# Two tiles of the branch projection's sum T2 trade places, and the two cache copies move behind the down projection's last residual addition

## The chip, the core and the metric

The kernel runs on one core of a Trainium2 chip. The core has five engines that each execute their own instructions in order: TensorE (PE) multiplies matrices, VectorE (DVE) and ScalarE (ACT) do elementwise work, GpSimd (POOL) and SyncE (SP) here do little but issue transfers. Transfers run on 16 DMA engines, which the queues of POOL (q0 in the profile) and SP (q1) share. Engines wait for each other through semaphores. The metric is the device time of one execution in microseconds (us), the median of several runs.

## The reference

One step of a hybrid decoder layer in float32, for a prompt of 1024 tokens and a decode batch of 8 x 8 tokens, 1088 columns in all; the model is 1024 wide, the feed-forward part 2816.

```
xn = RMSNorm(x)
q, k, v, glu_a, glu_b, gate_a, gate_b = split(xn @ w_in)
A = window_attention(q, k, v, sinks) @ w_o_attn            # window 128, caches k_past, v_past
c = LayerNorm(causal_conv31(glu_a * sigmoid(glu_b)))
B = silu(c) @ w_pb                                         # the branch projection
h = x + (sigmoid(gate_a) * A + sigmoid(gate_b) * B) @ w_out
gate, val = split(causal_conv3(RMSNorm(h) @ w_up))
y = h + (silu(gate) * val) @ w_down
outputs: RMSNorm(y); the last 128 keys and values of the prompt and of the decode batch; the convolutions' last rows
```

For the decode batch the new key and value windows are `concat(k_past, k_new)[-128:]`: 120 old positions are copied from the caches, and 8 are new. The copy of the old positions depends on nothing that the kernel computes.

## The kernel before, in words

A float32 product is made of three matmuls on reduced words: every operand is split into a high word (a cast on ACT, L227) and a low word (a subtraction on DVE, L228: the source less its cast), and `mm3` (L192 to L194) issues high x high, then the same weight with the data's low word, then the weight's low word. A "product" below is a run of such triples into one or two banks of PSUM, evicted by ACT or DVE.

The stages follow one another: the input projection, convolution and attention; the attention's out projection (`do_o`), the branch projection, the out projection, the up projection with its convolution (`ffn_up`), and the down projection (`ffn_down`). A scheduler that orders the rows of each engine when the kernel is built, from the program and its dependencies, sets the order of the work. `issue_after(x)` says that an instruction stands behind x.

*The branch projection.* Two output blocks are computed as seven products in place of eight, on sums of quarters of the data. `ln_apply` makes the sums T1 and T2 as words in SBUF and stores others to memory. `t_split` (L1048 to L1061) splits T1 to T3 into tiles called t{x}{j}{y}: x is the sum (0 is T1, 1 is T2, 2 is T3), j the half of the columns, y the word (0 high, 1 low). The tiles are allocated beforehand, in an order that a table gives:

```
at = {}
for tag in T_PLACES:
    at[tag] = self.t(tb, [P, KT // 2, QW], "t" + tag, F32R)
```

The order decides only at which place in SBUF a tile lies, and thus whose last use of that place it waits for. Some of the places were held before by `ma`, the gated result of the attention's out projection, which POOL stores to memory (L1011).

*The up projection.* It works through pairs of blocks, seven products a pair. `up_start(f)` prepares a row buffer `st` for the convolution: a memset and a copy on POOL (L1378, L1383), and, at f = 5 only, the two DMA copies of the caches between them (L1381, L1382). Each weight operand is split into `whi` and `wlo`, halves 0 and 1.

*The down projection.* `H`, the result, collects additions on DVE (L1690 in this part). `product(s, hooks)` works again in seven products for each row block m, on sums of the weights: `a_load` brings raw weights `ar` on SP's queue (L1631), `a_prep` adds two of them to `as` (L1644) and splits into `aw`, three products ahead (A_AHEAD = 3). `residual(m)` is a DMA on POOL's queue which adds the stored h to H:

```
def residual(m):
    nc.gpsimd.dma_start(H[:, m], self.d_h[m], accum_op=ALU.add)
```

`hooks` calls such steps at a place (m, p) of the product; the last two residuals (m = 3 and 7) are called at (0, 0) of `product(1)`.

Of the kernel before, what the change touches and what calls it, by code (L numbers as in the profile page):

```python
# [9 lines left out]
ALU = mybir.AluOpType  # L10
# [7 lines left out]
NT = 8  # L18
# [23 lines left out]
AHEAD = 3  # L42
UP_LATER = 100
GATE_AFTER = 30
T_PLACES = ("000", "001", "200", "201", "210", "100", "211", "111", "010", "011", "101", "110")
SPLIT_AFTER = 4
GATE_LATER = 60
DOWN = ((0, 1), (2, 3), (16, 17), (18, 19, 20, 21))
# [74 lines left out]
class Build:  # L123
# [898 lines left out]
    def phase_z(self, s_es, sp, xw, sb):  # L1022
# [40 lines left out]
# [3 lines that stand above are left out]
# [267 lines left out]
    def ffn_up(self, hh, hl, mp):  # L1333
        nc, tc, a, pool = self.nc, self.tc, self.a, self.pool
# [40 lines left out]
        def up_start(f):  # L1375
            st = self.t(ft, [P, FW], "st", bufs=4)
            ss = st[:, 2 + SEQ:].rearrange("p (b t) -> p b t", b=NB)
            z = nc.gpsimd.memset(st[:, 0:2], 0.0)  # L1378
            if f == 5:
                with tc.issue_after(z.ins):  # L1380
                    nc.gpsimd.dma_start(a["o_kwp"], a["kpT"][:, :, :, NT:])  # L1381
                    nc.gpsimd.dma_start(a["o_vwp"], a["vp"][:, NT:, :])  # L1382
            nc.gpsimd.tensor_copy(ss[:, :, 0:2], co[:, f, 2:].rearrange("p (b t) -> p b t", b=NB))  # L1383

            def parts(c):
                o, n = QUARTERS[c]
                m = min(n, SEQ - o)
                yield st[:, 2 + o:2 + o + m], lambda v: v[:, :m]
                if m < n:
                    yield ss[:, :, 2:], lambda v: v[:, m:n].rearrange("p (b t) -> p b t", b=NB)  # L1390

            def ev(c, o, n, ps):
                for d, r in parts(c):
                    nc.scalar.copy(d, r(ps))
            return st, ss, parts, ev
# [40 lines left out]
        def plain(f):  # L1436
            fs = (f, NF + f)
            ws = [self.weight(("up", x), 2 - n if f == 0 else 1) for n, x in enumerate(fs)] if f == 0 else [None] * 2
            both = [up_start(x) for x in fs]
            if f == 0:  # L1440
                for c in range(4):
                    for w, b in zip(ws, both):
                        self.stream(None, xs, b[3], chunks=(c,), w=w, table=QUARTERS)
            else:
                for x, b in zip(fs, both):
                    self.stream(("up", x), xs, b[3], chunks=range(4), table=QUARTERS)
            if f == 0:
                with self.later(-60):
                    sums()
            finish(f, both, PLAIN_LATER)  # L1450
# [75 lines left out]
        def pair(f):  # L1526
            base = 7 * (f - PLAIN)
            (_, _, pg, _), (_, _, pv, _) = both = [up_start(x) for x in (f, NF + f)]
            banks = {}
            copy = nc.scalar.copy  # L1530
# [82 lines left out]
    def ffn_down(self, mp):  # L1613
        nc, a = self.nc, self.a
        h_es, a_es, s_es, d_es = [ExitStack() for _ in range(4)]
        H = self.t(self.pool(h_es, "hd", "left"), [P, KT, T], "H")
# [17 lines left out]
        def a_prep(n):  # L1634
            add = nc.vector.tensor_tensor
            while len(tiles) < min(n, 56):
                p = len(tiles) % 7
                a11, a21, a12, a22 = raws[len(tiles) // 7]
                r = {0: a11, 5: a12, 6: a22}.get(p)
                if r is None:  # L1640
                    sums[p] = r = self.t(aw, [P, 3, P], "as", bufs=3)
                    x, y, op = ((a21, a22, ALU.add), (a11, sums.get(1), ALU.subtract), (a12, sums.get(2), ALU.add),
                                (a21, a11, ALU.subtract))[p - 1]
                    add(r, x, y, op)  # L1644
                t = self.t(aw, [P, 3, 2, P], "aw", F32R, bufs=A_AHEAD + 2)
                self.split_ps(t[:, :, 0, :], t[:, :, 1, :], r)
                tiles.append(t)
                a_load()
# [16 lines left out]
        gated = lambda f: self.g_split(f, self.g_load(f, row()), mp)  # L1665

        def residual(m):
            nc.gpsimd.dma_start(H[:, m], self.d_h[m], accum_op=ALU.add)

        seq = (("A", True, 0, 0), ("E", True, 4, 2), ("A", False, 0, 2), ("E", False, 0, 2), ("A", False, 4, 2),  # L1670
               ("C", True, 0, 0), ("A", False, 4, 0))
# [1 line left out]
        def product(s, hooks):  # L1673
            for m in range(4):
                banks = {}
                for p, (bank, fresh, row, c) in enumerate(seq):
                    n = 28 * s + 7 * m + p
                    a_prep(n + 1 + A_AHEAD)
                    w = tiles[n]
                    for j in range(2):  # L1680
                        if fresh:
                            banks[bank, j] = self.bank("mm" if bank == "A" else "aux")
                        ps = banks[bank, j][:, :QW]
                        cs = slice(j * QW, (j + 1) * QW)
                        for x in range(3):
                            b = ops[s, p, x]
                            self.mm3(ps, w[:, x, 0], w[:, x, 1], b[:, 0, cs], b[:, 1, cs], fresh and x == 0, x == 2,
                                     not fresh)
                        hs = H[:, row + m, (c + j) * QW:(c + j + 1) * QW]
                        self.added = nc.vector.tensor_tensor(hs, hs, ps, ALU.add).ins  # L1690
                    for go in hooks.get((m, p), ()):
                        go()

        def each(f, xs):
            return [lambda x=x: f(x) for x in xs]
# [25 lines left out]
        for m in range(3):  # L1721
            hooks.setdefault((m, 6), []).extend(each(residual, (m, m + 4)))
        product(0, hooks)
        late = {divmod(2 * x, KT): [lambda i=x + 10: second(i)] for x in range(11)}
        late[2, 2] = [lambda: a_prep(28 + A_AHEAD + 2)] + late[2, 2]
        self.down(2, H, None, late)
        product(1, {(0, 0): each(residual, (3, 7)), (2, 0): [unit], (2, 2): [unit], (2, 4): each(gated, (18,)),
                    (2, 6): each(gated, (19,)), (3, 0): each(gated, (20,)), (3, 1): [unit] + each(gated, (21,)),
                    (3, 2): [unit]})
        a_es.close()  # L1730
# [191 lines left out]
```

## Time and profile before

| | us |
|---|---|
| median of 3 runs | 1653.63 (1653.21 to 1654.59) |
| profiled execution | 1655.33 |
| its span | 1653.5 |
| PE busy | 1641.8 (99%) |
| DVE busy | 1372.9 (83%) |
| ACT busy | 865.5 (52%) |
| POOL busy | 260.3 (16%) |
| mean granted PE clock | 0.998 |

The profile lists, for the profiled execution, groups of instructions by engine, line of the program, operation and tile names (output<-input, buffer numbers left out), with their busy time, and the idle time of the engine before them with the instruction that ended it. A row of a timeline gives the start, the duration, the engine, the line, and in brackets the idle time before and its releaser. A row of a window gives busy times of PE, PE's weight loads, DVE, ACT and POOL with the counts of instructions, then the granted clock, the share of the 16 DMA engines and GB/s. Matmuls overlap, so two starts lie closer than one duration. A store or load is shown at its issue; "DMA to landing" is the time from the issue until it has arrived.

### The profile page before, as it was taken

The page shows a single profiled execution, that of the slowest core. Times are in us where ns is not written, and L with a number is a line of the kernel's source. Part 1 is how long each engine was busy: PE and PEld are TensorE (multiplying, and loading weights), DVE is VectorE, ACT ScalarE, POOL GpSimd, SP SyncE. Part 2 cuts the span into 40 slices and gives each one's busy share as a digit, 9 for nine tenths or more (in the row PEclk, how much of TensorE's full clock was granted, in tenths as well). Part 3 has the DMA queues.
Part 4 walks back from the last instruction along what each step waited for, and adds up shares of the span by engine and source line. Part 5 has one row for each costly group of instructions (what it writes and reads, how often), then busy time and mean ns, then how long its engine had stood idle before and what let it go on. Part 6 is the DMA issues. An engine that isn't in the chain of part 4 may idle for free. (4 is left out here: it accounts for less than half of the span.)

```text
span 1653.5 us, 30189 instructions
## 1 busy us (share of the span) xinstructions
PE 1641.8 (99%) x11606; PEld 1625.1 (98%) x11606; DVE 1372.9 (83%) x2474; ACT 865.5 (52%) x1795; POOL 260.3 (16%) x551
## 2 busy tenths in 40 slices
PE   9999999999999999999999999999999999999998
PEld 9999999999999999999999999999999999999997
DVE  7899979999979996787755887698888787989867
ACT  6524378774488845585533454454444454524222
POOL 0100112221011111121003421142222110000000
PEclk9999999999999999999999999999999999999999
DMA  6221222223121255647763533243333334766403
GB/s 209 84 66 47 65 71 75 94 98 96 51 61 45 86 204 178 199 162 195 194 223 105 186 110 127 77 137 114 116 109 115 98 100 135 259 162 164 109 14 109
DMA packets 102497, 200.48 MB, mean 121 GB/s; under 512 B 23904, under 2 KB 54640, under 8 KB 102336
## 3 DMA queue, kind: packets, MB, share of 16 engines
q1 hardware_dynamic: 78864, 128.52, 25.0%
q0 software_dynamic: 23056, 69.75, 14.2%
q8 instruction: 91, 1.49, 0.4%
q14 instruction: 54, 0.44, 0.1%
q10 hardware_dynamic: 432, 0.27, 0.1%
HBM read 136.44 MB, written 64.03 MB: 121 GB/s over the span
## 5 line engine op out<-in xcount | busy, mean ns | idle before, releaser
L192 PE MATMUL mm<-xh,whi 128*128 128x384 f32 (+1 forms) x904 | 301.3, 333 | 0.0
L193 PE MATMUL mm<-xl,whi 128*128 128x384 f32 (+1 forms) x904 | 295.4, 327 | 0.2
L194 PE MATMUL mm<-xh,wlo 128*128 128x384 f32 (+1 forms) x904 | 295.5, 327 | 0.0
L193 PEld LDWEIGHTS mm<-xl,whi 128*128 128x128 f32 x904 | 170.0, 188 | 1.6 <-DVE xl L279 0.8
L192 PEld LDWEIGHTS mm<-xh,whi 128*128 128x128 f32 x904 | 169.9, 188 | 0.7
L194 PEld LDWEIGHTS mm<-xh,wlo 128*128 128x128 f32 x904 | 169.7, 188 | 0.1
L1403 DVE SCALAR_TENSOR_TENSOR acc<-st,fc,acc 128x1104 f32<-128x1104 f32 x88 | 119.9, 1364 | 3.7 <-ACT acc L1401 2.4
L173 ACT CAST whi<-wraw 128x1024 fp32r<-128x1024 f32 (+1 forms) x65 | 62.7, 970 | 72.9 <-PE mm L193 52.7
L227 ACT CAST whi<-wraw 128x512 fp32r<-128x512 f32 x84 | 52.6, 626 | 77.0 <-PE aux L194 36.9
L227 ACT CAST wlo<-wraw 128x512 fp32r<-128x512 f32 x84 | 52.6, 626 | 73.5 <-PE aux L194 41.3
L522 DVE SCALAR_TENSOR_TENSOR bt<-u,consts,bt 128x513 f32<-128x513 f32 x120 | 89.7, 747 | 0.7
L522 DVE SCALAR_TENSOR_TENSOR c<-sm,hsum,c 128x512 f32<-128x512 f32 x120 | 89.5, 746 | 0.7
L192 PE MATMUL mm<-mh,whi 128*128 128x272 f32 (+4 forms) x296 | 88.2, 298 | 0.0
L194 PE MATMUL mm<-mh,wlo 128*128 128x272 f32 (+4 forms) x296 | 87.9, 297 | 0.0
L228 DVE TENSOR_TENSOR wlo<-wraw,wlo 128x512 fp32r<-128x512 f32 x84 | 60.7, 723 | 29.0 <-ACT wlo L227 27.8
L522 DVE SCALAR_TENSOR_TENSOR c<-u,consts,c 128x512 f32<-128x512 f32 x112 | 83.5, 746 | 0.6
L193 PE MATMUL mm<-ml,whi 128*128 128x272 f32 (+4 forms) x280 | 82.9, 296 | 0.0
L228 DVE TENSOR_TENSOR whi<-wraw,whi 128x512 fp32r<-128x512 f32 x84 | 58.2, 694 | 28.3 <-ACT whi L227 27.2
L174 DVE TENSOR_TENSOR wlo<-wraw,whi 128x1024 fp32r<-128x1024 f32 (+1 forms) x65 | 72.6, 1121 | 8.6 <-ACT whi L173 7.2
L1555 ACT COPY st<-mm 128x272 f32<-128x272 f32 (+2 forms) x140 | 46.8, 350 | 54.4 <-PE mm L194 54.4
L192 PE MATMUL aux<-mh,whi 128*128 128x272 f32 (+4 forms) x232 | 69.7, 300 | 0.0
L193 PE MATMUL mm<-tl,wlo 128*128 128x272 f32 x240 | 69.6, 290 | 0.0
(652 smaller groups left out, 5741.3 us busy)
## 6 DMA issues: line engine op xcount, KB each, us to landing
wraw<-wall SPq DMA_DIRECT2D x118, 512.0 KB, 4.2
bw<-d_b SPq DMA_DIRECT2D x42, 272.0 KB, 4.0
d_b<-gd POOLq DMA_DIRECT2D x36, 272.0 KB, 6.1
d_b<-acc POOLq DMA_DIRECT2D x24, 272.0 KB, 3.7
ar<-wdn SPq DMA_DIRECT2D x32, 192.0 KB, 3.5
d_g<-acc POOLq DMA_DIRECT2D x10, 544.0 KB, 5.0
ga<-d_ga SPq DMA_DIRECT2D x8, 544.0 KB, 4.8
ct<-d_c SPq DMA_DIRECT2D x8, 544.0 KB, 5.6
```

Source lines behind the costliest of these rows:

```text
L173: self.cast = self.nc.scalar.copy(h[:, z], r[:, z]).ins
L174: self.nc.vector.tensor_tensor(l[:, z], r[:, z], h[:, z].bitcast(F32), ALU.subtract)
L192: mm(ps, wh, xh, start=first, stop=False, skip_group_check=more)
L193: mm(ps, wh, xl, start=False, stop=False, skip_group_check=more)
L194: self.last_mm = mm(ps, wl, xh, start=False, stop=last, skip_group_check=more).ins
L227: self.cast = self.nc.scalar.copy(h, src).ins
L228: self.low = self.nc.vector.tensor_tensor(l, src, h.bitcast(F32), ALU.subtract).ins
L522: mac = lambda o, x, w: nc.vector.scalar_tensor_tensor(o, x, w, o, ALU.mult, ALU.add)
L1403: nc.vector.scalar_tensor_tensor(acc, st[:, k:k + AW], fw(f, k), acc, ALU.mult, ALU.add)
L1555: op(d, r(ps))
```

## The change: what it does

Three edits: in the table of places, T2's low word of the second half (`111`) and T3's (`211`) trade their positions; the two cache copies leave `up_start`; and they are issued by a new hook behind the residual of row block 7, on the same queue. Lines after the first removed ones shift by four (L1644 is L1640 in the new program, L1690 is L1686).

```diff
-T_PLACES = ("000", "001", "200", "201", "210", "100", "211", "111", "010", "011", "101", "110")
+T_PLACES = ("000", "001", "200", "201", "210", "100", "111", "211", "010", "011", "101", "110")
...
         def up_start(f):
             st = self.t(ft, [P, FW], "st", bufs=4)
             ss = st[:, 2 + SEQ:].rearrange("p (b t) -> p b t", b=NB)
-            z = nc.gpsimd.memset(st[:, 0:2], 0.0)
-            if f == 5:
-                with tc.issue_after(z.ins):
-                    nc.gpsimd.dma_start(a["o_kwp"], a["kpT"][:, :, :, NT:])
-                    nc.gpsimd.dma_start(a["o_vwp"], a["vp"][:, NT:, :])
+            nc.gpsimd.memset(st[:, 0:2], 0.0)
             nc.gpsimd.tensor_copy(ss[:, :, 0:2], co[:, f, 2:].rearrange("p (b t) -> p b t", b=NB))
...
         def residual(m):
-            nc.gpsimd.dma_start(H[:, m], self.d_h[m], accum_op=ALU.add)
+            self.rest = nc.gpsimd.dma_start(H[:, m], self.d_h[m], accum_op=ALU.add).ins
...
-        product(1, {(0, 0): each(residual, (3, 7)), (2, 0): [unit], (2, 2): [unit], (2, 4): each(gated, (18,)),
+
+        def windows():
+            with self.tc.issue_after(self.rest):
+                nc.gpsimd.dma_start(a["o_kwp"], a["kpT"][:, :, :, NT:])
+                nc.gpsimd.dma_start(a["o_vwp"], a["vp"][:, NT:, :])
+
+        product(1, {(0, 0): each(residual, (3, 7)) + [windows], (2, 0): [unit], (2, 2): [unit], (2, 4): each(gated, (18,)),
```

DVE's rows in the branch projection, where the low words of T2 are written; the names are tile, buffer number and, in brackets, what a row waits for (DMASW is the landing of a POOL transfer, DMAHW of an SP transfer, Activation is ACT):

```order
 L228 TENSOR_TENSOR t101_1039_7959<-w1_942_7286,t100_1034_7954 128x4x136 [waits Activation_49]
-L228 TENSOR_TENSOR t111_1036_7956<-w2_975_7547,t110_1040_7960 128x4x136 [waits DMASW7_49,DMASW5_49,Activation_49]
-L228 TENSOR_TENSOR t111_1036_7956<-w3_1005_7786,t110_1040_7960 128x4x136 [waits Activation_49]
+L228 TENSOR_TENSOR t111_1035_7955<-w2_975_7547,t110_1040_7960 128x4x136 [waits DMASW5_49,Activation_49]
+L228 TENSOR_TENSOR t111_1035_7955<-w3_1005_7786,t110_1040_7960 128x4x136 [waits Activation_49]
 L228 TENSOR_TENSOR wlo1_1049_7990<-wraw_1010_7833,wlo1_1049_7990 128x512 [waits Activation_49]
```

The rows keep their order, and t111 loses its wait for one of two POOL transfers. Ten rows on, T3's low word has it:

```order
-L228 TENSOR_TENSOR t211_1035_7955<-mh11_1026_7943,t210_1033_7953 128x544 [waits DMAHW0_49,Activation_49]
-L228 TENSOR_TENSOR t211_1035_7955<-mh11_1026_7943,t210_1033_7953 128x544 [waits Activation_49]
+L228 TENSOR_TENSOR t211_1036_7956<-mh11_1026_7943,t210_1033_7953 128x544 [waits DMAHW0_49,DMASW7_49,Activation_49]
+L228 TENSOR_TENSOR t211_1036_7956<-mh11_1026_7943,t210_1033_7953 128x544 [waits Activation_49]
 L228 TENSOR_TENSOR whi1_1058_8103<-wraw_1010_7833,whi1_1058_8103 128x512 [waits PE_49,Activation_49]
```

So the wait has moved with the place. In the up projection, in the pair of blocks behind the copies, PE's rows are these before, at the end of the product on the weight tile `wlo0_1364`:

```order
L193 MATMUL aux_1379_11817<-tl01_1237_10195,wlo0_1364_11677 128x272
L194 MATMUL aux_1379_11817<-th01_1229_10187,wlo0_1364_11677 128x272
L192 MATMUL aux_1386_11931<-mh01_1196_9665,wlo0_1380_11832 128x272 [waits DVE_49,Activation_49]
L193 MATMUL aux_1386_11931<-ml01_1198_9667,wlo0_1380_11832 128x272
L192 MATMUL aux_1387_11945<-mh11_1205_9821,wlo0_1380_11832 128x272 [waits DVE_49]
```

The product on `wlo0_1380`, which is a further tile of the name wlo0, follows at once. The same place of the new program, and 72 rows on:

```order
L193 MATMUL aux_1379_11815<-tl01_1237_10195,wlo0_1364_11675 128x272
L194 MATMUL aux_1379_11815<-th01_1229_10187,wlo0_1364_11675 128x272
L192 MATMUL mm_1375_11770<-th10_1230_10188,whi1_1367_11707 128x272 [waits Activation_49]
...
L193 MATMUL mm_1376_11784<-tl21_1241_10199,whi0_1377_11798 128x272
L194 MATMUL mm_1376_11784<-th21_1233_10191,whi0_1377_11798 128x272
L192 MATMUL aux_1386_11929<-mh01_1196_9665,wlo0_1380_11830 128x272
L193 MATMUL aux_1386_11929<-ml01_1198_9667,wlo0_1380_11830 128x272
```

Three products (on whi1_1367, wlo1_1374 and whi0_1377) now stand between the two, which is the order that every other pair has before and after. Last, the end of POOL's rows, before:

```order
L1668 DMA H_15734<-d_h_64 128x1088 [waits DMASW5_49,DVE_49]
L1668 DMA H_15734<-d_h_64 128x1088 [waits DMASW6_49,DVE_49]
L1668 DMA H_15734<-d_h_64 128x1088 [waits DMASW7_49,DVE_49]
L1668 DMA H_15734<-d_h_64 128x1088 [waits DMASW0_49,DVE_49]
L1901 UNCONDITIONAL_BRANCH
```

and after:

```order
L1664 DMA H_15732<-d_h_64 128x1088 [waits DMASW5_49,DVE_49]
L1664 DMA H_15732<-d_h_64 128x1088 [waits DMASW6_49,DVE_49]
L1726 DMA o_kwp<-kpT 2048x120 [waits DMASW7_49]
L1727 DMA o_vwp<-vp 8x2x15360 [waits DMASW0_49]
L1903 UNCONDITIONAL_BRANCH
```

The copies stand behind the eighth residual as the last transfers on POOL; each waits for an older POOL transfer whose semaphore it uses again (the one eight transfers before it). SP's rows have the same order in both programs.

## The prediction

> **What bounds the kernel now.** I read the busy times first, then the list of what TensorE (PE) waited for, then timelines of each engine around those waits, and last the transfers around the place to which the copies go.
>
> ```profile
> PE 1641.8 (99%) x11606; PEld 1625.1 (98%) x11606; DVE 1372.9 (83%) x2474; ACT 865.5 (52%) x1795; POOL 260.3 (16%) x551
> ...
> PE mm L193 <- DVE t L228: 1.6, 1, 1.6
> ...
> PE aux L192 <- ACT wlo L227: 0.8, 1, 0.8
> ```
>
> PE is busy for 99% of the span and no matmul is added or removed. So the time moves only where PE stops, and an edit elsewhere counts as far as it opens or closes a stop. The two waits quoted (instruction, whom it waited for, then total, times and longest in us) are the ones that the change can touch. Of the other five one is the second step of the first stop below, and four stand where order and waits stay as they are.
>
> **The stop at T2.** PE's timeline (start, duration, instruction, and in brackets idle time and releaser), then windows of it (busy times, then PE's clock, DMA share and GB/s):
>
> ```profile
> 745.02 0.29 PE L194 MATMUL aux<-t,whi 128*128 128x272 f32 x1
> ...
> 745.78 0.29 PE L192 MATMUL mm<-t,wlo 128*128 128x272 f32 x1
> 747.63 0.39 PE L193 MATMUL mm<-t,wlo 128*128 128x272 f32 x1 [1.56 <-DVE t L228]
> 748.23 0.39 PE L194 MATMUL mm<-t,wlo 128*128 128x272 f32 x1 [0.21 <-DVE wlo L228]
> 748.46 0.29 PE L192 MATMUL mm<-t,wlo 128*128 128x272 f32 x1
> ...
> 749.70:752.90 3.20, 3.20 (x16) 3.20 (x15) 3.20 (x6) 3.20 (x8) 0.40 (x1) 0.50 0.54 165
> ```
>
> From 745.02 to 745.78 the starts are six steps apart, 0.127 us each. The next three starts come 1.85, 0.60 and 0.23 us apart, so 1.72 + 0.47 + 0.10 = 2.3 us are lost. Two microseconds later the granted clock is 0.50 for 3.2 us: 16 matmuls take 3.2 us instead of 16 x 0.127 = 2.0, a loss of 1.2, or of 1.6 if I take half of the 3.2. I take 1.4. The stop costs 3.7 us together.
>
> Who is late there? VectorE (DVE), ScalarE (ACT) and GpSimd (POOL), with the landing times of the two stores:
>
> ```profile
> 743.26 0.71 DVE L228 TENSOR_TENSOR t<-w,t 128x544 fp32r<-128x544 f32 x1
> 746.22 1.36 DVE L228 TENSOR_TENSOR t<-w,t 128x544 fp32r<-128x544 f32 x2 [2.25 <-ACT ml L1153]
> 747.50 0.68 DVE L228 TENSOR_TENSOR wlo<-wraw,wlo 128x512 fp32r<-128x512 f32 x1
> ...
> 738.99 2.29 ACT L227 CAST t<-w 128x544 fp32r<-128x544 f32 x4 [0.49 <-DVE ma L1010]
> ...
> 738.22 0.56 POOL L1011 DMA_DIRECT2D d_ma<-ma  x1 [2.29 <-DVE ma L1010]
> ...
> DMA to landing us min/median/max: 4.3/4.3/4.3
> ...
> 739.74 0.61 POOL L1011 DMA_DIRECT2D d_ma<-ma  x1
> ...
> DMA to landing us min/median/max: 6.4/6.4/6.4
> ```
>
> DVE stands idle for 2.25 us before it writes T2's low part t111. The releaser named is ACT, but the casts that t111 needs (four in one row) were done by 741.3. What ends at that moment is a store: `ma` issued at 739.74 lands 6.4 later, at 746.1, and t111 lies where that `ma` lay. So DVE waits for a store to leave the place, and PE waits for DVE.
>
> **The change, part by part.**
>
> *T2 and T3 trade places.* No instruction is added or moved; one wait goes from t111's row to that of T3's low part t211. t111 keeps its wait for the earlier store (738.22 + 4.3 = 742.5) and for the casts, both over when DVE ends the row of 743.26. So the two t111 halves start at about 743.9 and 744.5 and the row of wlo follows at 745.2 and ends near 745.85, just ahead of PE, which would ask for it from 745.9 to 746.05. t211 comes after the rows quoted, later than 746.1, so its new wait should cost nothing; if T3 came earlier, it would inherit the stop. I take a gain of 3.6 of the 3.7 (0.1 for a wlo that comes a touch late); the least is 2.3, if a small stop or the clock loss stays.
>
> *The copies leave POOL's row between two memsets.* A stop in the up projection, 46 us behind the copies, belongs to this edit:
>
> ```profile
> 1063.68 0.29 PE L194 MATMUL aux<-th,wlo 128*128 128x272 f32 x1
> 1064.73 0.39 PE L192 MATMUL aux<-mh,wlo 128*128 128x272 f32 x1 [0.76 <-ACT wlo L227]
> 1064.96 0.29 PE L193 MATMUL aux<-ml,wlo 128*128 128x272 f32 x1
> ...
> 1065.21 0.29 PE L193 MATMUL aux<-ml,wlo 128*128 128x272 f32 x1
> 1065.46 0.39 PE L194 MATMUL aux<-mh,wlo 128*128 128x272 f32 x1
> ...
> 1064.06 0.62 ACT L227 CAST wlo<-wraw 128x512 fp32r<-128x512 f32 x1 [2.40 <-PE aux L194]
> ...
> 1066.00:1070.00 4.00, 4.00 (x34) 4.00 (x34) 4.00 (x4) 1.85 (x4) 0.93 (x2) 1.00 0.47 135
> ```
>
> PE loses 0.92 + 0.10 + 0.13 = 1.15 us up to 1065.46, and about 0.1 behind it: 1.25. The product that starts at 1064.73 uses wlo0_1380, which lies where wlo0_1364 lay, and PE's order (shown with the change) has it right behind the product on wlo0_1364. So ACT's cast into that place waits 2.40 us for the last matmul of that product, and PE waits for the cast. In the new order three products of 24 matmuls, some 9 us at 0.127 each, stand between the two, and the cast has that time. The clock stayed at 1.00 here, so nothing more is to be had. I take 1.25 (0.9 to 1.3). Taking the copies out of this place saves nothing else, since PE has no other stop beside it.
>
> *The copies come behind the last residual.* What they cost the 16 DMA engines is seen where they stand now:
>
> ```profile
> 1018.10 1.08 POOL L1381 DMA_DIRECT2D o_kwp<-kpT  x1 [0.40 <-issue]
> 1019.17 0.57 POOL L1382 DMA_DIRECT2D o_vwp<-vp  x1
> ...
> DMA to landing us min/median/max: 10.9/10.9/10.9
> ...
> q0 software_dynamic: 324, 1.63, 89.0%
> ```
>
> The last row is POOL's own queue from 1019 to 1025: 89% of 6 us, 5.34 us of all engines, for 1.63 MB. Both copies are 2 x 960 KB = 1.97 MB, so 6.4 us of all sixteen. Now the new place:
>
> ```profile
> 1533.51 0.87 POOL L1668 DMA_DIRECT2D H<-d_h  x1 [2.64 <-DVE H L1606]
> ...
> 1538.00:1542.00 4.00, 4.00 (x34) 4.00 (x33) 3.81 (x8) 0.72 (x2) 0.00 (x0) 1.00 1.00 359
> 1542.00:1546.00 4.00, 4.00 (x34) 4.00 (x33) 3.63 (x9) 0.82 (x2) 0.00 (x0) 1.00 0.95 330
> ...
> q0 software_dynamic: 91, 0.39, 99.1%
> ...
> 1539.49 0.38 SPq L1631 DMA_DIRECT2D ar<-wdn  x1
> ...
> DMA to landing us min/median/max: 5.0/5.0/5.0
> ...
> 1545.19 0.56 DVE L1644 TENSOR_TENSOR as<-ar,ar 128x384 f32<-128x384 f32 x1
> ...
> 1550.17 0.43 DVE L1690 TENSOR_TENSOR H<-H,mm 128x272 f32<-128x272 f32 x1
> ...
> 1545.19:1550.60 5.41, 5.41 (x46) 5.41 (x45) 4.70 (x10) 1.03 (x2) 0.00 (x0) 1.00 0.29 89
> ...
> 1552.82 0.29 PE L192 MATMUL mm<-mh,aw 128*128 128x272 f32 x1
> ```
>
> The copies would be issued right behind the residual of 1533.51, near 1534.4 and 1535.5. The engines are full there until 1546 (shares 1.00 and 0.95). From 1536 to 1538 POOL's queue alone filled them (the 99.1%), though SyncE (SP) had weight loads waiting: what POOL issues first goes first, or at best takes turns. So the loads behind it move later by up to the 6.4 us. The load of `ar` issued at 1539.49 now lands at 1544.5, and DVE's sum at 1545.19 reads it, 0.7 later. With the copies ahead it lands at L = 1544.5 + 6.4 = 1550.9. DVE executes in order, so its additions of matmul results to H queue behind that sum. From the sum to the end of the addition of 1550.17 lie 4.70 busy us; PE needs the bank which that addition frees at 1552.82. PE then stops for L + 4.70 - 1552.82 = 2.8 us. Below L = 1548.1 it doesn't stop. Such a stop may cost clock as T2's did: 0 (as behind the 0.9 us gap above) to 1.4 (as at T2's 1.7 us); I take 0.7. The copies delay the other loads of SP too; I price that at nothing, because what those loads bring is used behind the additions already held up, and PE's lost time is counted once. If that cover fails, each further load costs what it is late beyond the first stop. POOL has nothing behind the copies, so their wait for the residual holds up nobody; nor do they reach the end, 110 us on.
>
> [...]
>
> **Sum.** -3.6 (T2) - 1.25 (up projection) + 2.8 (DVE held) + 0.7 (clock) = -1.35. The durations come from the profiled execution of 1655.3 us (span 1653.5); the runs without profile have a median of 1653.63, and I set the difference against that: 1652.3 us.
>
> **Rivals.**
> 1. *The copies stay hidden.* Their packets take turns with SP's, or they trickle, as where they stand now, where the second landed only after 10.9 us and no PE stop followed; L stays below 1548.1. Against it: 0.7 us of slack and full engines. Gain 3.6 + 1.25 = 4.85: 1648.8.
> 2. *T2's stop shrinks only.* wlo's low part ends 0.05 to 0.2 us before it is needed; a late store or a DVE that loses a little on the way keeps a stop of some 1.5 us with its clock loss. Then only about 1.5 of the 3.6 is won: 1652.3 + 2.1 = 1654.4, no change to measure.
> 3. *The held load is much later: slower.* If `ar` is held not by 6.4 but by the 10.9 us which the second copy took from issue to landing, L = 1555.4, PE stops 7.3 us and loses 1.4 of clock: -4.85 + 8.7 = +3.85, 1657.5. Break-even lies at L = 1551.6 (a stop of 3.45 and 1.4 of clock); slower by 0.2% needs L = 1554.9. Against it: in 6.4 us the copies are through, however they are mixed.
>
> **How the numbers follow.** About 0.2%, 3.3 us, is what a measurement of this kernel can tell from no change. The forecast (a new stop eats most of the gain) gets 0.55, with its own range 1650.4 to 1653.7: stops of 1.6 to 3.5 us with and without the clock loss. Rival 1 gets 0.30, rival 2 0.10, rival 3 0.05. Faster: rival 1 and a little of the forecast, 0.33. Slower: rival 3, 0.05. The rest, 0.62, is no change. The range for eight in ten reaches down to rival 1 with both gains in full (3.7 + 1.3), 1648.6, and up beyond the forecast's own upper end to the near part of rival 2, 1654.0.
>
> **What the profile after would show.** T2: no wait of PE for `t`, a clock of 1.00 near 750, t111 written at 743.9. Up projection: no wait of PE for wlo. Copies: two DMA rows behind the last H<-d_h; an `ar` load with over 10 us to landing; a DVE idle of some 5 us before L1640 and a PE wait for `H` of 2 to 3 us near 1548 in the new count. I am wrong if DVE isn't held there (the copies cost nothing), or if a PE wait for T3's tile appears (the stop has only moved).

## The result: 0.25% slower

The changed kernel takes 1657.35 us (median of 16 runs, 1655.75 to 1660.39), the kernel before 1652.99 us (16 runs, 1651.72 to 1656.35). The ratio is 1.0025, with a 95% interval of 1.0018 to 1.0033, that is 3 to 5.5 us more. (The ratios here and below are those on record for the runs; they lie near the quotient of the two medians, and aren't the same number.) The forecast was 1652.3, with 1648.6 to 1654.0 as range: wrong in direction, and outside the range.

### The profile page after: what moved, and what is told of

Read it like the earlier page. It is cut to its first block, busy times and chain, and to the rows that moved or that the text cites. A ratio compares the mean times of both kernels' runs of the same rounds, so it can differ in the third digit from the quotient of the medians.

```text
span 1655.6 us, 30197 instructions
## 1 busy us (share of the span) xinstructions
PE 1642.0 (99%) x11606; PEld 1625.7 (98%) x11606; DVE 1372.4 (83%) x2474; ACT 864.6 (52%) x1795; POOL 259.5 (16%) x551
## 5 line engine op out<-in xcount | busy, mean ns | idle before, releaser
L193 PE MATMUL mm<-tl,whi 128*128 128x272 f32 x240 | 69.6, 290 | 0.0
```

Of the source, the lines that this page charges most:

```text
L193: mm(ps, wh, xl, start=False, stop=False, skip_group_check=more)
```

## The profile after

The profiled execution has a span of 1655.6 us (1657.41 with what lies around it). First the busy times and the waits of TensorE (PE) that answer to those of before:

```profile
PE 1642.0 (99%) x11606; PEld 1625.7 (98%) x11606; DVE 1372.4 (83%) x2474; ACT 864.6 (52%) x1795; POOL 259.5 (16%) x551
...
PE mm L192 <- DVE H L1686: 3.9, 1, 3.9
...
PE aux L192 <- DVE H L1686: 0.5, 1, 0.5
```

Both waits that the change aimed at (for T2's tile and for wlo in the up projection) are gone. In their place one wait for an addition to H on VectorE (DVE) has come, of 3.9 us. The second line is an old one, 0.3 before.

T2 in the changed kernel, PE's timeline and DVE's:

```profile
745.67 0.29 PE L192 MATMUL mm<-t,wlo 128*128 128x272 f32 x1
745.80 0.29 PE L193 MATMUL mm<-t,wlo 128*128 128x272 f32 x1
745.92 0.30 PE L194 MATMUL mm<-t,wlo 128*128 128x272 f32 x1
...
743.18 1.99 DVE L228 TENSOR_TENSOR t<-w,t 128x544 fp32r<-128x544 f32 x3
745.09 0.68 DVE L228 TENSOR_TENSOR wlo<-wraw,wlo 128x512 fp32r<-128x512 f32 x1
```

PE goes on in steps of 0.13 us, and DVE's three low words and wlo follow one another without idle time, as the prediction worked out (wlo ends at 745.77). Now the new stop. GpSimd (POOL) and SyncE (SP), the landing of the load of `ar`, DVE, PE, and a window (columns as in the prediction's windows):

```profile
1528.69 0.85 POOL L1664 DMA_DIRECT2D H<-d_h  x1 [2.67 <-DVE H L1602]
1529.55 1.10 POOL L1726 DMA_DIRECT2D o_kwp<-kpT  x1
1530.62 0.62 POOL L1727 DMA_DIRECT2D o_vwp<-vp  x1
...
1534.67 0.38 SPq L1627 DMA_DIRECT2D ar<-wdn  x1
...
DMA to landing us min/median/max: 12.7/12.7/12.7
...
1539.78 0.56 DVE L228 TENSOR_TENSOR aw<-as,aw 128x384 fp32r<-128x384 f32 x1 [0.15 <-ACT aw L227]
1547.49 0.56 DVE L1640 TENSOR_TENSOR as<-ar,ar 128x384 f32<-128x384 f32 x1 [7.15 <-DMA ar<-wdn]
...
1547.88 0.29 PE L194 MATMUL aux<-ml,aw 128*128 128x272 f32 x1
1552.06 0.56 PE L192 MATMUL mm<-mh,aw 128*128 128x272 f32 x1 [3.90 <-DVE H L1686]
1552.42 0.43 PE L193 MATMUL mm<-mh,aw 128*128 128x272 f32 x1
...
1552.30:1557.80 5.50, 5.50 (x26) 5.50 (x27) 3.03 (x7) 0.51 (x1) 0.00 (x0) 0.51 0.25 72
```

The load of `ar` takes 12.7 us instead of 5.0, so it is 7.7 late. DVE stands before the sum of L1640 for 7.15 us, its additions to H stand behind that, and PE stops: 4.18 - 0.13 = 4.05 us between two starts, 0.23 at the next. Then the clock is 0.51 for 5.5 us, with 26 matmuls where 5.5 / 0.127 = 43 would go: 2.2 us. The new stop costs 6.5 us in this execution, at the place and through the chain that the prediction named, but with 3.5 forecast.

In the two profiled executions the account is short: the span goes from 1653.5 to 1655.6, which is -3.8 at T2, -1.25 in the up projection, +6.5 here, and 0.7 of small differences elsewhere. But the medians differ by 4.4, twice as much. So either T2 is worth less in the other runs, or the copies cost more in them.

## Experiments: is the stop at T2 always there?

**The swap alone.** Theory A: the profiled execution of before was a slow example. Theory B: T2's stop is always there, and the copies cost more than the trace shows.

```diff
-T_PLACES = ("000", "001", "200", "201", "210", "100", "211", "111", "010", "011", "101", "110")
+T_PLACES = ("000", "001", "200", "201", "210", "100", "111", "211", "010", "011", "101", "110")
```

> T2's and T3's tiles trade places, the copies stay in the up projection. Theory A (the profiled execution of before was a slow example: it lies 2.3 us over the median of its 16 runs, because T2's stop or its clock loss is smaller in most runs): the profile shows no PE wait for t, but the median falls by only 1 to 2 us. Theory B (the stop at T2 is the same 3.7 us in every run, and the copies cost more at their new place than the trace of the changed kernel shows): the median falls by 3.5 to 4. In both the wait of 0.8 us for wlo in the up projection stays.

Measured: 1651.95 us against 1652.81, ratio 0.9991 (0.9983 to 1.0000): 0.9 us by the medians, 1.5 by the ratio and at most 2.8 by the interval, which holds theory A's 1 to 2 and not theory B's 3.5 to 4. PE has no wait for t, and the wait for wlo (0.8) is there as before. The 3.6 that I took for T2 doesn't show in the median.

**The copies alone.** The changed kernel with the table of before.

> The copies move behind the last residual, the places stay as before. Both theories: PE stops about 4 us for H's addition, because the load of ar lands about 8 us late, the clock falls to 0.5 behind it for 5 us, and the up projection has no wait for wlo. Theory A: the median rises by 5.3 to 5.9 (6.6 to 7 less 1.25). Theory B: by 7.5 to 8.

Measured: 1658.34 us (6 runs, 1655.85 to 1662.14, the profiled one the fastest), ratio 1.0032 (1.0019 to 1.0045), 5.5 us above before. That is theory A's number; with the swap's -0.9 it makes +4.6, and the change as a whole measured +4.4. The more telling thing is in the profile. T2's tiles stand as before in this kernel, and yet its waits hold none for t:

```profile
PE mm L192 <- DVE H L1686: 3.9, 1, 3.9
PE mm L653 <- DVE warm L646: 1.1, 1, 1.1
PE aux L420 <- ACT pth L227: 0.8, 1, 0.8
PE aux L568 <- DVE sm L560: 0.2, 1, 0.2
```

Why? The last `ma` store, for which t111 waits, lands after 3.9 us here and after 6.4 in the profiled execution of before. SP and POOL of the kernel before, then of this one:

```profile
739.41 0.80 SPq L1044 DMA_DIRECT2D mh<-d_t  x2
...
739.74 0.61 POOL L1011 DMA_DIRECT2D d_ma<-ma  x1
```

```profile
740.77 2.48 SPq L1044 DMA_DIRECT2D mh<-d_t  x3
...
739.88 0.61 POOL L1011 DMA_DIRECT2D d_ma<-ma  x1
...
DMA to landing us min/median/max: 3.9/3.9/3.9
```

SP reloads T3's words (`mh<-d_t`) as soon as the store that wrote them has landed. That store took 4.2 us from its issue in the first case, and 5.4 in the second. In the first the reload goes out 0.33 us ahead of the `ma` store, which then lands late; in the second it goes out 0.9 behind. So the stop at T2 would be decided by which of two transfers is issued first, within one microsecond.

**Forcing the order.** Before's table and copies, but the reloads on POOL's own queue, where they stand behind the two stores of `ma`:

```diff
-                nc.sync.dma_start(stage[x, j], self.d_t[x - 2, j])
+                nc.gpsimd.dma_start(stage[x, j], self.d_t[x - 2, j])
```

> The kernel before, but the four reloads mh<-d_t (L1044) go on POOL's queue, behind the two stores of ma, instead of SP's; places and copies as before. Theory: T2's stop comes only in the executions in which the reload on SP's queue, released when the d_t store lands, goes out ahead of the last ma store (739.41 against 739.74 in the profiled execution of before; 740.77 against 739.88 in that of the kernel with the copies alone, which had no stop). With the reloads behind the store there is never a stop: the profile has no PE wait for t, ma lands 4 us after its issue, and the time is that of the kernel with the swap alone, 0.5 to 1.5 below before. Rival (the place itself makes T2 late): the stop stays.

Measured: 1651.32 us against 1653.27, ratio 0.9986 (0.9977 to 0.9995), a gain of 2 by the medians with the interval from 0.8 to 3.8; the swap's interval, 0 to 2.8, overlaps it. POOL's rows with the landing of that store, and then all of this kernel's waits of PE:

```profile
739.35 0.61 POOL L1011 DMA_DIRECT2D d_ma<-ma  x1
739.89 1.15 POOL L1044 DMA_DIRECT2D mh<-d_t  x2
...
DMA to landing us min/median/max: 3.7/3.7/3.7
```

```profile
PE mm L653 <- DVE warm L646: 1.1, 1, 1.1
PE aux L420 <- ACT pth L227: 0.8, 1, 0.8
PE aux L192 <- ACT wlo L227: 0.8, 1, 0.8
```

T2's stop is gone with the tiles at their old places. The place alone doesn't make it; the order of the reload and the store does.

**The kernel before, three more times.**

> The kernel before once more, for one more profile of it. If the stop at T2 is there in some executions alone, this one has either the 2.3 us with the clock loss, with the reload ahead of the last ma store, or less than 0.4 us and the reload behind it.

> The kernel before once more, for a profile of it. It has T2's stop of 2 us or more where the reload mh<-d_t goes out ahead of the last ma store, and less than 0.4 us where it goes out behind.

> As the run ahead of it: the kernel before, with the stop where the reload is ahead of the store, without it otherwise. Over all profiles of kernels in which the tiles stand as before, some have the stop and some not.

What the profiles of the tiles' old places show, with the time that PE lost between 745 and 757 (starts further apart than one step of 0.127, added up), and the issues of the reload and the store:

| execution | time, us | lost at T2, us | reload | last `ma` store |
|---|---|---|---|---|
| profile of before | 1655.33 | 3.8 | 739.41 | 739.74 |
| again, first | 1655.42 | 3.0 | 739.72 | 740.16 |
| again, second | 1653.05 | 0.35 | 742.65 | 741.70 |
| again, third | 1653.90 | 2.1 | 739.73 | 739.95 |
| copies alone | 1655.85 | 0.3 | 740.77 | 739.88 |

Reload first: a stop, three times. Store first: none, twice. All fourteen profiles of this case, those with the tiles swapped too, divide in the same way: in the seven with the reload first the last `ma` store lands after 5.9 to 7.0 us, in the other seven, the forced order among them, after 3.7 to 5.4. The changed kernel and the swap alone are among the first seven (6.3 us each) and have no stop at T2, so the swap does take the late store out of PE's way. The four times of before less what was lost at T2 are 1651.5, 1652.4, 1652.7 and 1651.8, and the swap alone has a median of 1651.95. The profile on which I built was the worst of the four at this place. The second has lost time elsewhere instead (1.5 us ahead of a small product near 720), so the order isn't independent of what happened earlier in the execution; how often each order comes in runs without a profile stays open, and with it what the stop costs in the median.

## Experiments: what do the copies hold up?

**Without the copies.**

```diff
-        def windows():
-            with self.tc.issue_after(self.rest):
-                nc.gpsimd.dma_start(a["o_kwp"], a["kpT"][:, :, :, NT:])
-                nc.gpsimd.dma_start(a["o_vwp"], a["vp"][:, NT:, :])
...
-        product(1, {(0, 0): each(residual, (3, 7)) + [windows], (2, 0): [unit],
+        product(1, {(0, 0): each(residual, (3, 7)), (2, 0): [unit],
```

> The changed kernel without the two copies: the 120 old positions of the sample's key and value windows aren't written. If the copies' transfers are the whole cause of the stop, DVE isn't held, no PE wait for H over 0.5 us and no clock loss near 1550. Theory A: 2.3 to 3.3 below before. Theory B: 4.7 to 5 below.

Measured: 1650.92 us against 1652.81, ratio 0.9986 (0.9978 to 0.9995), 1.9 below. DVE isn't held (the sum of L1640 follows at its usual distance) and the longest wait for H is 0.5:

```profile
PE mm L653 <- DVE warm L646: 1.1, 1, 1.1
PE aux L420 <- ACT pth L227: 0.8, 1, 0.8
PE aux L192 <- DVE H L1686: 0.5, 1, 0.5
PE aux L568 <- DVE sm L560: 0.3, 1, 0.3
```

So the copies at their new place cost 1657.35 - 1650.92 = 6.4 us by the medians, near the 6.5 of the profile. (In the profile of the copies alone, with the same stop, the place cost 5.6; see the last section.) Theory A holds and theory B doesn't: no hidden cost of the copies, a smaller gain at T2. The 1.9 is less than the 2.3 that A asked at least, but its interval (0.8 to 3.6) holds that and not B's 4.7. The step from the swap alone to this kernel, 1651.95 to 1650.92, is 1.0, about the up projection's 1.25.

**The copies one at a time.** I had put the load's delay at 6.4 us, the time that both copies take of sixteen engines; it was 7.7. Each kernel leaves out one of the two copies at the new place.

> The changed kernel with only the keys' copy behind the last residual; the values' copy is left out, so the old positions of the values' window aren't written. Theory P (the load of ar is late by the DMA time of what is ahead of it, whatever its shape): 3.5 to 4 us late of the 7.8 with both copies, L near 1548, PE stops 0 to 0.6 us, no clock loss, time 2 us below before as without copies. Theory Q (the packets of the values' copy, 16 of 61 KB that each hold one engine for 2.3 us, cost the loads more than their share): the keys' copy alone delays ar by its share or less, no stop.

> The same with only the values' copy; the old positions of the keys' window aren't written. Theory P: ar 2.5 to 3 us late, no stop. Theory Q: ar 4 us late or more, PE stops 0.4 us or more.

The landing of the same `ar` load, DVE's idle time before the sum, and PE's wait, with the keys' copy alone:

```profile
DMA to landing us min/median/max: 7.9/7.9/7.9
...
1542.48 0.56 DVE L1640 TENSOR_TENSOR as<-ar,ar 128x384 f32<-128x384 f32 x1 [2.28 <-DMA ar<-wdn]
```

and with the values' copy alone:

```profile
DMA to landing us min/median/max: 9.8/9.8/9.8
...
1544.80 0.56 DVE L1640 TENSOR_TENSOR as<-ar,ar 128x384 f32<-128x384 f32 x1 [4.23 <-DMA ar<-wdn]
...
PE mm L192 <- DVE H L1686: 1.0, 1, 1.0
```

Against 5.0 the keys cost the load 2.9 us and PE nothing: 1650.64 us against 1653.27, ratio 0.9982 (0.9973 to 0.9992). The values, with the same number of bytes, cost it 4.8 and PE 1.0: 1651.79 us against 1653.27, 0.9984 (0.9975 to 0.9993). The two sum to the 7.7. What held the load is not the bytes alone: that is theory Q's outcome, and its reason, the size of the packets, is tested below. While the values' large packets are under way (none starts in this stretch, from 1537.6 to 1539), SP's queue has only half of the engines' time, although nothing else runs:

```profile
q1 hardware_dynamic: 137, 0.25, 46.7%
```

Of those packets (16 of 61,440 B, 2.3 us each) the trace has two waves of eight in flight from 1535 to 1539, never more, and of the keys' packets sixteen and more. By these counts the values' copy would run on eight engines, two packets on each, 4.6 us in a row, and a load that spreads over sixteen (in the profile of before SP's loads alone filled all of them, 101.3% from 1539.3 to 1545) would be done when the slow eight are. My 6.4 had averaged over sixteen engines, where the half that is busy counts. It was also read off at the old place, where the packets took longer: at the new one the keys' packets take 2.7 us of sixteen engines, near the 2.9 measured, and the values' 2.3, which is 4.6 on eight, near the 4.8. A mean would have given 5.0.

**The values in smaller packets.** The first test of the packets' size, at the same place:

```diff
-                nc.gpsimd.dma_start(a["o_vwp"], a["vp"][:, NT:, :])
+                for y in range(2):
+                    nc.gpsimd.dma_start(a["o_vwp"][:, :, y * P:(y + 1) * P], a["vp"][:, NT:, y * P:(y + 1) * P])
```

> The changed kernel with the values' copy as two DMAs of 128 columns each, rows of 512 B instead of 16 stretches of 61 KB; the same bytes at the same place. Theory Q (the large packets hold ar longer than their share: 4.8 us with the values alone against 2.85 with the keys alone): ar is some 5.7 us late instead of 7.8, PE stops about 2 us instead of 4.1, and the time falls by 2 to 4 below that of the changed kernel. Theory P (only the bytes ahead count): ar stays 7 to 8 us late and the time stays within 1 of it.

Measured: 1652.88 us against 1653.74, ratio 0.9997 (0.9987 to 1.0007). The load lands after 10.5 us, 5.5 late, and PE waits 1.7 us with the clock at 1.00. The delay and the stop are those of theory Q, but they don't show it: POOL issued the first half at 1533.99, in the same moment as the load (1533.96), and the second only at 1539.91, so that half of the bytes at most stood in the load's way; and those alone cost it 5.5 - 2.9 = 2.6 us, no less for a byte than the large packets (4.8 for all of them). Some eight packets were in flight here as well. Byte for byte the smaller packets delayed the load no less, so their size is not the cause; that this kernel is faster than the changed one would be the work of the half that goes out late.

**The values over sixteen engines.** One DMA again, the same bytes, but with an outer dimension of 128 in place of 8:

```diff
-                nc.gpsimd.dma_start(a["o_vwp"], a["vp"][:, NT:, :])
+                rows = lambda t: t.rearrange("b s k -> b (s k)").rearrange("b (x y) -> x b y", y=240)
+                nc.gpsimd.dma_start(rows(a["o_vwp"]), rows(a["vp"][:, NT:, :]))
```

> The changed kernel with the values' copy read and written in another order: 128 x 8 stretches of 240 numbers (960 B) in one DMA, the same bytes at the same place. Theory R (the values' copy as it was keeps only eight of the sixteen DMA engines busy, each for two packets of 2.3 us, 4.6 us in a row, and a load needs all sixteen, so that it is late by the 4.6 of the slow half and not by the mean of 2.3; in two columns of 128 it was still on eight): if the new order spreads it over sixteen (up to 16 of its packets in flight, as the keys' copy has), ar is 5.2 to 5.8 us late instead of 7.8, PE stops 1.5 to 2.2 us instead of 4.1, and the time is 2 to 4 below that of the changed kernel. Rival (only the bytes on POOL's queue ahead of ar count): ar stays 7 to 8 us late, PE stops 3.5 to 4.5, and the time stays.

Measured: 1654.0 us (10 runs) against 1652.61, ratio 1.0007 (0.9997 to 1.0017), less than half of the change's +0.25%. Up to 16 of the packets (now 4,800 B) are in flight. The load, DVE, and PE's wait:

```profile
DMA to landing us min/median/max: 10.7/10.7/10.7
...
1546.68 0.56 DVE L1640 TENSOR_TENSOR as<-ar,ar 128x384 f32<-128x384 f32 x1 [5.14 <-DMA ar<-wdn]
...
PE mm L192 <- DVE H L1686: 1.9, 1, 1.9
```

It is 5.7 late instead of 7.7, and PE loses 2.0 us without a loss of clock: theory R. (The time is a little over that of the smaller packets, although the stop is alike; this profile has a further stop of 1.2 us in the branch projection, at 758.9, of which the others have at most 0.4. What makes it stays open.) In these traces the most packets of the values' copy in flight were eight with an outer dimension of 8, and sixteen with 128. What sets that number isn't shown.

**The copies where nothing waits.** The changed kernel, with the copies on SP's queue behind the last load of `ar`:

```diff
-                        nc.sync.dma_start(r, rows[:, :, y, :])
+                        self.rest = nc.sync.dma_start(r, rows[:, :, y, :]).ins
...
-                nc.gpsimd.dma_start(a["o_kwp"], a["kpT"][:, :, :, NT:])
-                nc.gpsimd.dma_start(a["o_vwp"], a["vp"][:, NT:, :])
+                nc.sync.dma_start(a["o_kwp"], a["kpT"][:, :, :, NT:])
+                nc.sync.dma_start(a["o_vwp"], a["vp"][:, NT:, :])
...
-        product(1, {(0, 0): each(residual, (3, 7)) + [windows], (2, 0): [unit],
+        product(1, {(0, 0): each(residual, (3, 7)), (2, 0): [unit],
...
-                    (3, 2): [unit]})
+                    (3, 2): [unit, windows]})
```

(The residuals no longer set `self.rest`.)

> The copies go on SP's queue behind the last load of ar, near 1550, where the DMA engines have nothing to do until 1586. If what costs is only the traffic ahead of the ar loads, this is as fast as without copies, within 0.5 us (theory A: 2.3 to 3.3 below before, theory B: 4.7 to 5). If a DRAM copy beside the down projection costs by itself (memory ports, PE's clock), it lies between that and the changed kernel.

Measured: 1650.60 us (11 runs, 1649.98 to 1651.66) against 1652.81, ratio 0.9984 (0.9975 to 0.9992). It is faster than both kernels, and no slower than the one without copies (1650.92). SP's timeline and the windows:

```profile
1549.71 0.62 SPq L1726 DMA_DIRECT2D o_kwp<-kpT  x1
1550.38 1.40 SPq L1727 DMA_DIRECT2D o_vwp<-vp  x1
...
1548.00:1556.00 8.00, 8.00 (x66) 8.00 (x65) 5.73 (x13) 2.06 (x4) 0.00 (x0) 1.00 0.85 233
1556.00:1564.00 8.00, 8.00 (x66) 8.00 (x65) 6.25 (x14) 1.64 (x4) 0.00 (x0) 1.00 0.16 65
```

The same bytes fill the engines (0.85) 20 us later beside a PE that doesn't notice (66 matmuls in 8 us, clock 1.00). The cost was the traffic ahead of one load, not a copy beside matmuls. (This edit changes the queue as well as the place; which of the two is needed wasn't tried apart.)

## Why the prediction was wrong, point by point

The chains of waits held, and the steps that failed are sizes in the sum: T2's gain, taken at 3.6 and worth 0.9 by the medians, and the delay of the `ar` load, taken at 6.4 and measured at 7.7, with the stop (2.8, measured 4.3) and the clock behind it (0.7, measured 2.2).

- *What bounds the kernel*, right: PE at 99%, and every difference lies in its stops. Of each edit the direction was right as well.
- *T2, gain 3.6*: the mechanism held in the profiled execution (PE lost 3.8 there and nothing after), and t211's new wait cost nothing. The term was mis-sized: I took what one execution lost for what every run loses. With the swap alone the median falls by 0.9 (1.5 by the ratio, at most 2.8). What decides it, the reload's issue against the store's, is on no list of waits. But the profiled 1655.33 lay 1.7 over the median that the sum was set against (2.3 over that of the 16 runs); the prediction named both numbers and didn't ask which stop made the difference.
- *Up projection, gain 1.25*, right: 1.25 between the two traces, 1.0 between the medians. The three products now between the two wlo tiles do it.
- *Copies, PE stops 2.8*: the chain was right to the instruction (`ar`, the sum at L1640, the additions, the third product), and so was its formula: the stop is the load's delay less 3.6 (0.7 of slack ahead of the sum, 2.2 between the addition's end and PE's need, and 0.7 of short waits that DVE no longer has), so 7.7 - 3.6 = 4.1, measured 4.05 (and 0.23 behind it). The delay was mis-sized: 6.4, an average over sixteen engines (and, with the packets' times at the new place, even 5.0), where one of the copies never had more than eight packets in flight, in two waves of 2.3 us. With sixteen in flight the delay was 5.7.
- *Clock, 0.7*: 2.2 in the profiled execution. I had taken the middle between 0 and 1.4, and the loss after the longer stop exceeded both. The size isn't fixed: the profile of the copies alone lost a microsecond less behind the same stop.
- The terms missed by some 2.7 (T2), 1.5 (stop) and 1.5 (clock), and 0.2 (up projection): 5.9 on the good side. The sum forecast -1.35 and +4.4 came, a miss of 5.7.
- *Rivals*: the third, slower, is what came, in its direction and for its reason of a load held longer than 6.4. That its 1657.5 nearly equals the measured 1657.35 is luck: it had a stop of 7.3 us (4.3 came) and took the 3.6 at T2 as won. It was given 0.05 with the argument that in 6.4 us the copies are through, however they are mixed. That sentence failed: in the changed kernel's trace their packets run from 1534.7 to 1544.3. The first rival (copies hidden) is refuted at this place and true 20 us later; the second is not seen: in every profile with the swap wlo came in time or at most 0.2 us late.

## What to carry to other kernels

A stop that hangs on which of two transfers goes out first may be there in one profile and absent in the next (here 3.8 us lost in one of the kernel before and 0.35 in another), so look at the spread of the runs, and take two or three profiles before a term is built on one stop. Price a transfer ahead of another by the engine that is busy longest, not by the mean share of all: the values' copy, with an outer dimension of 8 and at most eight packets in flight, made the load 4.8 us late, where the mean over sixteen engines was 2.3. And a copy that nobody waits for belongs behind the last load that somebody waits for, not in front of it (here 1650.60 us against 1657.35).

## What the runs showed of the hardware that I had not expected

The granted clock doesn't follow the length of a stop alone. In the profile of before, a gap of 1.7 us at T2 was followed by a clock of 0.50 for 3.2 us. In the first repetition of before the gap at the same place was 2.3 us, and the clock stayed:

```profile
746.00:749.00 3.00, 0.88 (x6) 0.50 (x4) 1.76 (x3) 0.93 (x2) 0.00 (x0) 1.00 0.80 236
749.00:752.00 3.00, 2.79 (x22) 2.74 (x22) 3.00 (x7) 1.81 (x4) 0.00 (x0) 1.00 0.42 160
752.00:756.00 4.00, 4.00 (x33) 3.94 (x32) 4.00 (x8) 4.00 (x9) 0.91 (x1) 1.00 0.65 172
```

A gap of 2.0 us (values over sixteen engines) cost no clock either (1.00 from 1549 to 1557). And one and the same stop can cost more or less of it. Behind the 3.9 us wait for H the clock stayed low twice as long in the changed kernel as in the kernel with the copies alone, where the place cost 5.6 us in place of 6.6 (summed over PE's starts):

```profile
1550.80:1557.60 6.80, 5.54 (x24) 5.57 (x25) 4.47 (x11) 0.51 (x1) 0.00 (x0) 0.50 0.20 58
...
1551.70:1555.10 3.40, 3.40 (x17) 3.40 (x17) 2.06 (x5) 0.00 (x0) 0.00 (x0) 0.50 0.36 98
```

The three slow stretches inside these executions last 3.4 us (before, 749.6 to 753.0), 3.4 (the copies alone) and 6.8 (the changed kernel). Why a 1.7 us gap is followed by one and a 2.3 us gap isn't stays open. How long PE was idle doesn't tell the two apart: in the profile of before it was idle for 1.6 us of the 3.4 ahead of the fall (746.2 to 749.6), and in the first repetition for 2.1 us of the 3 from 746 to 749 (the row above, 3.00 less 0.88), and there no fall followed.
